# Row maximum over 64 MB: four blocks with pitches of their own, and some rows by TensorE and GpSimd

## The chip, the cores and the metric

The kernel runs on one core of a Trainium2 chip. The metric is the device time of one execution in microseconds; the comparison is by medians of several executions.

## The reference

The input is `x`, float32, 32 x 512 x 1024, drawn from a normal distribution. The output is the maximum over the last axis:

```python
def reference(x):
    return np.max(x, axis=-1).astype(np.float32)      # (32, 512)
```

Flattened, these are 16,384 rows of 1,024 numbers, 4 KB each: 67.11 MB are read, 65 KB are written, and each number is looked at once.

## The kernel before

The 16,384 rows are dealt out to the 128 partitions so that each partition has 128 rows which lie together in memory (`xr`). Neighbouring partitions are therefore 128 x 4 KB = 512 KB apart in HBM. This distance is called the pitch here.

The loop over `ROWS` (27 entries, 10 and 13 rows at first, single rows at last) does three things for each entry `g`. It takes `g` places in `ring`, a tile of 46 rows per partition, and goes back to place 0 when they don't fit. It issues one load of `g` rows for all partitions from the queue of SyncE (SP), line 47. It issues one `reduce_max` on VectorE (DVE), line 48, which writes `g` columns of `res`. A load waits on SP until the instructions that read its places before have finished; a reduce waits for its load. SP and DVE each work in the order of the program, so nothing overtakes anything on either queue.

The last row is loaded and reduced in two halves (lines 58 and 59), which are joined by one small instruction (line 60). The results leave by two stores from the queue of ScalarE (ACT): the first 112 columns at line 53 as soon as they are there, the last 16 at line 64. TensorE (PE) has nothing to do, and GpSimd (POOL) only sets four constants at the start.

Of the kernel before, what the change touches and what calls it, by code (L numbers as in the profile page):

```python
# [1 line left out]

# [4 lines left out]


F32 = mybir.dt.float32


ROWS = [10, 13, 12, 10, 9, 8, 7, 7, 6, 5, 5, 4, 4, 3, 3, 3, 3, 2, 2, 2, 2, 2, 1, 1, 1, 1, 1]
RING = 46


@with_exitstack
def kernel(
    ctx: ExitStack,
    tc: tile.TileContext,
    x: bass.AP,  # L20
    out: bass.AP,
):
    nc = tc.nc
    P = 128
    X = mybir.AxisListType.X

    xf = x.flatten_outer_dims()
    N, D = xf.shape
    H = D // 2
    I = N // P  # L30

    xr = xf.rearrange("(p i) d -> p i d", p=P)
    of = out.flatten_outer_dims()
    out_r = bass.AP(tensor=of.tensor, offset=of.offset, ap=[[I, P], [1, I]])

    once = ctx.enter_context(tc.tile_pool(name="once", bufs=1))
    ring = once.tile([P, RING, D], F32)
    res = once.tile([P, I], F32)
    part = once.tile([P, 2], F32)

    b = at = 0
    stored = 0
    for g in ROWS:
        if at + g > RING:
            at = 0
        xc = ring[:, at:at + g, :]
        nc.sync.dma_start(out=xc, in_=xr[:, b:b + g, :])
        nc.vector.reduce_max(out=res[:, b:b + g], in_=xc, axis=X)  # L48
        at += g
        b += g  # L50
        if not stored and b >= I - 16:
            stored = b
            nc.scalar.dma_start(out=out_r[:, :b], in_=res[:, :b])

    assert b == I - 1 and at + 1 <= RING
    for h in range(2):
        xh = ring[:, at, h * H:(h + 1) * H]
        nc.sync.dma_start(out=xh, in_=xr[:, b, h * H:(h + 1) * H])
        nc.vector.reduce_max(out=part[:, h:h + 1], in_=xh, axis=X)  # L59
    nc.vector.tensor_tensor(  # L60
        out=res[:, b:b + 1], in0=part[:, 0:1], in1=part[:, 1:2],
        op=mybir.AluOpType.max,
    )
    nc.scalar.dma_start(out=out_r[:, stored:], in_=res[:, stored:])


# [1 line left out]
_INS = ['x']  # L68
_OUTS = [((32, 512), 'float32')]


# [23 lines left out]
```

## Time and profile before

| what | value |
|---|---|
| median of 8 executions | 166.87 us (166.26 to 167.31) |
| the profiled execution, its own time | 167.04 us |
| its span | 165.3 us |
| DVE busy | 139.4 us, 84% of the span, 30 instructions |
| bytes read | 67.11 MB, a mean of 406 GB/s over the span |

The span is what the profile covers; the own time has 1.74 us more, which lie around it. A busy share is an average over the whole span, so it doesn't tell which resource sets the pace of a stage. That is read from the waits and from the chain that ended last.

### The profile page before, as it was taken

What the parts mean: (1) busy time and instruction counts of PE and PEld (TensorE: products, weight loads), DVE (VectorE), ACT (ScalarE), POOL (GpSimd) and SP (SyncE); (2) the same over time, 40 slices, a digit from 0 to 9 for tenths busy, and PEclk for the clock granted to TensorE, in tenths of its full rate; (3) what the DMA queues carried; (4) which work ended last, traced back from release to release, by engine and by line L of the source; (5) the groups of instructions that cost most, each with busy time, mean ns of one, the idle gap of its engine ahead of it and who ended that gap; (6) DMA issues with size and microseconds to landing.
All of it is one profiled execution on the core that took longest, in us unless ns stands there. A gap on an engine that the chain in (4) does not pass through costs nothing.

```text
span 165.3 us, 118 instructions
## 1 busy us (share of the span) xinstructions
DVE 139.4 (84%) x30; POOL 0.2 (0%) x4
## 2 busy tenths in 40 slices
DVE  0001994399989999899999989999999999999994
POOL 0000000000000000000000000000000000000000
DMA  5999999989999999999999999999999999999970
GB/s 198 436 476 391 464 438 451 445 381 428 442 436 406 460 357 419 413 420 439 430 437 423 429 432 425 436 426 419 436 420 422 422 425 421 418 422 419 408 280 2
DMA packets 4464, 67.18 MB, mean 406 GB/s; under 512 B 752, under 2 KB 752, under 8 KB 1648
## 3 DMA queue, kind: packets, MB, share of 16 engines
q1 hardware_dynamic: 4176, 67.11, 95.6%
q10 hardware_dynamic: 288, 0.07, 0.2%
HBM read 67.11 MB, written 0.07 MB: 406 GB/s over the span
## 4 chain that ended last, share of the span: by engine, by line
DMA 70%; DVE 28%; issue 0%
DMA ring<-in_x_dram 70%; DVE res L48 27%; DVE part L59 1%; DVE res L60 0%
## 5 line engine op out<-in xcount | busy, mean ns | idle before, releaser
L48 DVE TENSOR_REDUCE res<-ring 128x2 f32<-128x2048 f32 (+11 forms) x27 | 138.1, 5165 | 23.5 <-DMA ring<-in_x_dram 23.3
L59 DVE TENSOR_REDUCE part<-ring 128x1 f32<-128x512 f32 x2 | 1.3, 675 | 0.0
L60 DVE TENSOR_TENSOR res<-part 128x1 f32<-128x1 f32 x1 | 0.2, 158 | 0.0
L79 POOL MEMSET const-uint8-127<- 128x1 uint8 x1 | 0.1, 103 | 0.0
L79 POOL MEMSET const-bfloat16-1.0<- 128x1 bf16 x1 | 0.1, 102 | 0.0
L79 POOL MEMSET const-float32-0.0<- 128x1 f32 x1 | 0.1, 99 | 0.2 <-issue 0.2
L79 POOL MEMSET const-float32-1.0<- 128x1 f32 x1 | 0.1, 99 | 0.0
## 6 DMA issues: line engine op xcount, KB each, us to landing
ring<-in_x_dram SPq DMA_DIRECT2D x2, 5120.0 KB, 35.5
ring<-in_x_dram SPq DMA_DIRECT2D x2, 3584.0 KB, 33.6
ring<-in_x_dram SPq DMA_DIRECT2D x1, 6656.0 KB, 30.3
ring<-in_x_dram SPq DMA_DIRECT2D x1, 6144.0 KB, 44.4
ring<-in_x_dram SPq DMA_DIRECT2D x4, 1536.0 KB, 38.9
ring<-in_x_dram SPq DMA_DIRECT2D x2, 2560.0 KB, 38.4
ring<-in_x_dram SPq DMA_DIRECT2D x5, 1024.0 KB, 22.2
ring<-in_x_dram SPq DMA_DIRECT2D x1, 4608.0 KB, 43.7
```

The costliest lines, as they stand in the source:

```text
L48: nc.vector.reduce_max(out=res[:, b:b + g], in_=xc, axis=X)
L59: nc.vector.reduce_max(out=part[:, h:h + 1], in_=xh, axis=X)
L60: nc.vector.tensor_tensor(out=res[:, b:b + 1], in0=part[:, 0:1], in1=part[:, 1:2], op=mybir.AluOpType.max,)
L79: nc = _bacc.Bacc("TRN2", target_bir_lowering=False, num_devices=1)
```

## The change

**Blocks.** The rows are cut into four blocks, by the code of 42, 36, 34 and 16 rows per partition (the short description names 42, 35, 34 and 17). Within a block each partition again has rows that lie together, so the pitch is 168, 144, 136 and 64 KB. Each block has a store of its own, from the ACT queue. The ring has 42 places in place of 46. The 25 loads are those in `BLOCKS`; the last row isn't halved any more.

**The other way.** Each entry `(n, m)` of `BLOCKS` is one load of `n` rows, of which the last `m` don't go to the large `reduce_max`. There are 14 such rows of 128: six loads of the first blocks carry 2, 2, 2, 2, 2 and 1 of them, three more carry 1 each. Such a row takes this way, in `by_gpsimd`:

```python
for c in range(C):                                  # C = 8
    nc.tensor.transpose(out=ps[:, c*P:(c+1)*P],
        in_=rows[:, k, c*P:(c+1)*P], identity=ident)          # L63, PE
nc.scalar.copy(out=sb, in_=ps)                                # L69, ACT
nc.gpsimd.partition_all_reduce(top, sb, P, bass_isa.ReduceOp.max)   # L71, POOL
...
nc.tensor.transpose(out=back[:, k, c:c + 1],                  # L76, PE, 8 of them
    in_=top[0:1, c*P:(c+1)*P], identity=ident[0:1, 0:1])
...
nc.vector.reduce_max(out=cols, in_=back, axis=X)              # L83, DVE
```

Eight 128 x 128 blocks are turned, so that the numbers of one row lie across the partitions; ACT takes them from PSUM to SBUF; POOL takes the maximum over the partitions; eight small transposes bring the result back to one number per partition and block, and a small `reduce_max`, called the merge from here on, takes the maximum of the eight. There are three `ps` buffers, and two each of `sb`, `top` and `back`.

The diff, cut to its core:

```diff
-ROWS = [10, 13, 12, 10, 9, 8, 7, 7, 6, 5, 5, 4, 4, 3, 3, 3, 3, 2, 2, 2, 2, 2, 1, 1, 1, 1, 1]
-RING = 46
+BLOCKS = [
+    [(14, 2), (14, 2), (14, 2)],
+    [(14, 2), (13, 2), (9, 1)],
+    [(7, 1), (8, 1), (6, 1), (5, 0), (3, 0), (3, 0), (2, 0)],
+    [(2, 0), (2, 0), (2, 0), (2, 0), (1, 0), (1, 0), (1, 0), (1, 0), (1, 0), (1, 0), (1, 0), (1, 0)],
+]
+RING = 42
...
+    at = first = 0
+    for loads in BLOCKS:
+        S = sum(n for n, m in loads)
+        xb = xf[first * P:(first + S) * P, :].rearrange("(p i) d -> p i d", p=P)
+        b = 0
+        for n, m in loads:
+            if at + n > RING:
+                at = 0
+            xc = ring[:, at:at + n, :]
+            nc.sync.dma_start(out=xc, in_=xb[:, b:b + n, :])
+            cols = res[:, first + b:first + b + n]
+            if m:
+                merge = by_gpsimd(xc[:, n - m:, :], cols[:, n - m:], m)
+            else:
+                run(backs)
+            nc.vector.reduce_max(out=cols[:, :n - m], in_=xc[:, :n - m, :], axis=X)
+            run(late)
+            if m:
+                late.append(merge)
...
+        late.append(store)
+        first += S
+    run(late)
```

The program is written with the merges and the small transposes put off by one load and one row. The instructions of the built kernel stand in another order, since its scheduler sorts them. On DVE and PE the built kernel has, for the first two loads (the others likewise):

```
DVE  L104 reduce of load 0, 12 rows    (waits for load 0)
     L83  merge of load 0              (waits for PE)
     L104 reduce of load 1, 12 rows    (waits for load 1)
     L83  merge of load 1              (waits for PE)
PE   L63  16 transposes of load 0      (waits for load 0)
     L76  8 + 8 small transposes of load 0   (each 8 wait for POOL)
     L63  16 transposes of load 1      (waits for load 1)
     L76  8 + 8 small transposes of load 1   (each 8 wait for POOL)
```

After the ninth merge DVE has 16 reduces of loads without a row for POOL: 5, 3, 3, five times 2, and eight times 1 row.

More of the change, by code (lines that the diff above doesn't have):

```diff
@@ L6 @@
 from concourse._compat import with_exitstack
+from concourse import bass_isa
+from concourse.masks import make_identity
 F32 = mybir.dt.float32
-ROWS = [10, 13, 12, 10, 9, 8, 7, 7, 6, 5, 5, 4, 4, 3, 3, 3, 3, 2, 2, 2, 2, 2, 1, 1, 1, 1, 1]
-RING = 46
+BLOCKS = [
[5 more added lines that the diff above has]
+RING = 42
 @with_exitstack
@@ L28 @@
     N, D = xf.shape
-    H = D // 2
+    C = D // P
     I = N // P
-    xr = xf.rearrange("(p i) d -> p i d", p=P)
     of = out.flatten_outer_dims()
-    out_r = bass.AP(tensor=of.tensor, offset=of.offset, ap=[[I, P], [1, I]])
     once = ctx.enter_context(tc.tile_pool(name="once", bufs=1))
+    turn = ctx.enter_context(tc.tile_pool(name="turn", bufs=2))
+    allr = ctx.enter_context(tc.tile_pool(name="allr", bufs=2))
+    psum = ctx.enter_context(tc.tile_pool(name="psum", bufs=3, space=bass.MemoryType.PSUM))
@@ L37 @@
+    psmall = ctx.enter_context(tc.tile_pool(name="psmall", bufs=2, space=bass.MemoryType.PSUM))
     ring = once.tile([P, RING, D], F32)
     res = once.tile([P, I], F32)
[L39 to L64, printed above, removed]
+    ident = once.tile([P, P], F32)
+    make_identity(nc, ident)
@@ new lines, with by_gpsimd, turn_back @@
+    backs = []
+    late = []
+    def by_gpsimd(rows, cols, m):
+        back = psmall.tile([P, m, C], F32)
+        for k in range(m):
+            ps = psum.tile([P, D], F32)
+            for c in range(C):
+                nc.tensor.transpose(
+                    out=ps[:, c * P:(c + 1) * P],
+                    in_=rows[:, k, c * P:(c + 1) * P],
+                    identity=ident,
+                )
+            sb = turn.tile([P, D], F32)
+            nc.scalar.copy(out=sb, in_=ps)
+            top = allr.tile([P, D], F32)
+            nc.gpsimd.partition_all_reduce(top, sb, P, bass_isa.ReduceOp.max)
+            run(backs)
+            def turn_back(top=top, k=k):
+                for c in range(C):
+                    nc.tensor.transpose(
+                        out=back[:, k, c:c + 1],
+                        in_=top[0:1, c * P:(c + 1) * P],
+                        identity=ident[0:1, 0:1],
+                    )
+            backs.append(turn_back)
+        return lambda: nc.vector.reduce_max(out=cols, in_=back, axis=X)
@@ new lines, in run, with store @@
+    def run(calls):
+        while calls:
+            calls.pop(0)()
+    at = first = 0
[12 more added lines that the diff above has]
+            else:
+                run(backs)
+            nc.vector.reduce_max(out=cols[:, :n - m], in_=xc[:, :n - m, :], axis=X)
+            run(late)
+            if m:
+                late.append(merge)
+            at += n
+            b += n
+        def store(first=first, S=S):
+            dst = bass.AP(tensor=of.tensor, offset=of.offset + first * P, ap=[[S, P], [1, S]])
+            nc.scalar.dma_start(out=dst, in_=res[:, first:first + S])
+        late.append(store)
+        first += S
@@ L68 @@
+    run(late)
+    assert first == I
 _INS = ['x']
```

## The prediction

> **What bounds the kernel now.** I read the page's first two parts and then the time by stages: is anything saturated, and where?
>
> ```profile
> span 165.3 us, 118 instructions
> ...
> DVE 139.4 (84%) x30; POOL 0.2 (0%) x4
> ...
> GB/s 198 436 476 391 464 438 451 445 381 428 442 436 406 460 357 419 413 420 439 430 437 423 429 432 425 436 426 419 436 420 422 422 425 421 418 422 419 408 280 2
> ```
>
> ```profile
> 8.00:20.00 12.00, 4.23 (x1) 0.00 (x0) 1.00 1.00 431
> 20.00:40.00 20.00, 15.08 (x2) 0.00 (x0) 1.00 1.01 437
> ...
> 60.00:80.00 20.00, 19.38 (x2) 0.00 (x0) 1.00 0.97 411
> ...
> 140.00:150.00 10.00, 9.67 (x5) 0.00 (x0) 1.00 1.01 421
> ```
>
> In the second view the last two columns are the DMA engines' busy share and GB/s. From 4 us to 159 us the share is 0.97 or more: the loads set the pace. DVE is nearly as full in the second half (19.4 us of 20). The chain that ended last says the same: loads, then in the last 9 us DVE with no wait.
>
> ```profile
> 133.72 19.91 DMA ring<-in_x_dram
> ...
> 153.65 7.92 DVE res L48 x6
> 161.57 1.20 DVE part L59 x2
> ...
> 162.79 0.16 DVE res L60
> ```
>
> Two series of numbers come from here. First, when rows land. The timeline has the second reduce starting at 31.5 us (23 rows landed) and the third at 46.05 us (35 rows), both right after a wait for a load:
>
> ```profile
> 31.51 14.02 DVE L48 TENSOR_REDUCE res<-ring 128x13 f32<-128x13312 f32 x1 [4.92 <-DMA ring<-in_x_dram]
> 46.05 23.68 DVE L48 TENSOR_REDUCE res<-ring 128x12 f32<-128x12288 f32 x2 [0.52 <-DMA ring<-in_x_dram]
> 97.06 43.72 DVE L48 TENSOR_REDUCE res<-ring 128x7 f32<-128x7168 f32 x9 [0.81 <-DMA ring<-in_x_dram]
> ```
>
> (46.05 - 31.51) / 12 = 1.21 us per row; 97.06 us is 76 rows, 1.24 from there. I use **landing of n rows = 3.6 + 1.22 n us** (23 rows: 31.7). Second, what a reduce costs, from the groups kept apart by shape (busy, mean ns):
>
> ```profile
> L48 DVE TENSOR_REDUCE res<-ring 128x7 f32<-128x7168 f32 x2 | 15.2, 7616 | 0.8 <-DMA ring<-in_x_dram 0.8
> ...
> L48 DVE TENSOR_REDUCE res<-ring 128x3 f32<-128x3072 f32 x4 | 13.3, 3348 | 0.5 <-DMA ring<-in_x_dram 0.3
> L48 DVE TENSOR_REDUCE res<-ring 128x12 f32<-128x12288 f32 x1 | 13.0, 12954 | 0.5 <-DMA ring<-in_x_dram 0.5
> L48 DVE TENSOR_REDUCE res<-ring 128x2 f32<-128x2048 f32 x5 | 11.2, 2280 | 0.3 <-DMA ring<-in_x_dram 0.3
> L48 DVE TENSOR_REDUCE res<-ring 128x5 f32<-128x5120 f32 x2 | 11.0, 5480 | 0.0
> ...
> L48 DVE TENSOR_REDUCE res<-ring 128x1 f32<-128x1024 f32 x5 | 5.7, 1209 | 0.0
> ```
>
> So a row costs DVE 1.08 us in a large reduce and 1.21 us alone, against 1.22 us to load it.
>
> **What the Trainium skill says.** (1) "DMA: Bandwidth & Descriptors", Latency and other measured facts: copies between HBM tensors ran at 207 GB/s per direction with a 512 KiB pitch, at 214 with a padded one. The same page (Where 436 GB/s comes from) puts a core's ceiling at 435 GB/s. The trace doesn't show the loss: 431 and 437 GB/s at a pitch of 512 KB from 8 to 40 us; it falls to 411-430 later, where loads are smaller and one stage waits for the ring. (2) "GPSIMD Engine Reference", 3.2: a partition-axis reduce of 128 x 2048 took 247.7 us; 3.1: a loop of many operations runs at about 3 per cycle, a tight one at 1.8 cycles per element. No run here shows either. (3) "SBUF — State Buffer" says that on trn2 `tensor_reduce` never contends with GpSimd for the shared port, so I charge DVE nothing for POOL's work; the trace before can't show it.
>
> **The change, part by part.**
>
> *Blocks and pitch.* At the ceiling of 435 GB/s the 67.11 MB take 154.3 us, at the mean of 8 to 159 us (about 425) 157.9 us. A gain of 0 to 3.6 us on the loads, hence on each landing at most 2%. It counts only where DVE waits for loads at the end. I take 0. Two more stores: 0.4 us of ACT's queue each, beside other work. The last store has 16 columns as before, and the time from DVE's end to the span's end stays 165.3 - 162.95 = 2.35 us.
>
> *Work taken from DVE.* 14 rows at 1.08 = 15.1 us, less nine merges of about 0.2 us (line 60, the nearest small row, is 0.16), less what single rows cost more. DVE has about 127 us of work in place of 139.4. Off the path while loads set the pace.
>
> *Work added.* For each row of the other way:
> - 8 transposes. The skill ("TensorE: Matmul & The Clock Gate", Part 4) has 275 to 390 ns for one; in a stream they may overlap, so 0.9 to 3.1 us a row. I take 2.0.
> - The copy: "ScalarE: Activation LUTs" (What ACT_TABLE_LOAD costs) gives 186 ns + 0.833 ns per element, 1.04 us. The table load comes before the first landing.
> - POOL, **the number that decides, T**. From below: 1024 elements at 1.8 cycles and 1.2 GHz, 1.5 us. From above: half of 247.7, 124 us. My estimate from the same page: 16 lanes to one needs four steps of a move and a maximum (8 operations), with read, write and the exchange between cores about 14 per element, 4.7 cycles at the full 3 per cycle. A real loop will need 6 to 9: 5.1 to 7.7 us. I take the middle and 0.1 for dispatch, **T = 6.5 us**. The first call may pay about 6 us more (2.1), but POOL is free from some 10 us on and its first input comes at 24 us.
> - 8 small transposes: 0.5 to 2.2 us, taken as 1.0.
>
> *The wait that is added.* In the built order the merge of a load stands on DVE **ahead of** the next load's reduce, and PE's small transposes stand ahead of the next load's transposes. So DVE can't start the next reduce until POOL is done with this load, and the next load's POOL work can't start earlier either: the rows go round one circle, PE, ACT, POOL, PE, DVE. Its length: 2.0 + 1.04 + 1.0 + 0.2 + 0.2 for hand-overs = 4.4 us (3 to 6), plus T per row (a second row's transposes and copy lie under the first's T). That is **17.4 us for two rows, 10.9 for one**. The reduce of 12 rows, 13.0 us, lies inside it. Against it stand the landings, 17.1 us for 14 rows, 15.9 for 13, and then 11.0, 8.5, 9.8, 7.3 for 9, 7, 8, 6. So the circle keeps up at first and then falls behind. Start of a load's work is the later of its landing and the merge before:
>
> 20.7 (load 0 landed); merges at 38.1, 55.5, 72.9, 90.3, 107.7 (two rows each), then 118.6, 129.5, 140.4, 151.3. The ninth's rows had landed at 3.6 + 99 x 1.22 = 124.4. DVE then has 29 rows left, all but a few long landed (the last at 159.8): 5.48 + 2 x 3.35 + 5 x 2.28 + 8 x 1.21 = 33.3 us. DVE ends at 184.6, the span at 187.0, own time + 1.74 = 188.7. The profiled execution before was 0.17 above the median: **188.5 us**.
>
> *The ring.* SP now waits for PE as well as DVE. Tightest is the load of 8 rows, which needs the reduce of load 4 (90.3 + 11.9 = 102.2), while loads already issued last until 2 + 85 x 1.22 = 105.7. For a longer T the loads stall, but what is late next is DVE's queue anyway, so this costs nothing further.
>
> **Rivals.** *POOL is quick* (T up to 2 us). Then circles fit inside the reduces, and DVE sets the end from the landing of 93 rows (117.1): 7.6 + 5.5 + 0.4 + 33.3 = 163.9, time 167.8; with landings at 435 GB/s (1.205 us a row) 166.4, or less if small loads gain too. This ends at no change or slightly faster. For it: the page's 1.8 cycles for the simplest body. Against it: a maximum across lanes isn't that. It decides below about 2 us; at 3.4 us the last circles already are 7.8 long and the time is 170. *POOL is slow:* T = 9 gives circles of 22.4 and 13.4, 20.7 + 112 + 53.6 + 33.3 + 3.9 = 223.5; at the partition-axis price, 124 us, 14 rows give 1.8 ms. *The pitch does nothing:* likely, given 437 GB/s before, and it changes no sum above since DVE is late.
>
> **How the numbers follow.** The circle with T of 5 to 8: 0.87; POOL quick or nearly so: 0.07; POOL slow: 0.06. Ends: T = 5 gives 177 (the circle keeps up until load 4), T = 7.7 gives 205; the 4.4 us, nine times, may be 1.5 off either way, 13 us. Not all errors fall together: 174 to 207. By 0.3%, about what a measurement here can tell: faster 0.04, same 0.03, slower 0.93.
>
> **What would show it.** POOL at about 14 x 6.5 us busy; DVE idle before L83, released by PE, and that by POOL; DVE's last 33 us without waits; loads done well before the end. It's wrong if DVE's idle time before L83 is small, or if its last reduces wait for loads.

## The result, and the profile after

The changed kernel is slower, by far less than forecast: **168.63 us** (median of 11) against 166.55 us (median of 32 runs of the kernel before, the earlier eight among them); ratio 1.0124, 95% interval 1.0106 to 1.0142. In a later comparison on one chip it was 168.49 against 165.86 us, 1.016 (1.0146 to 1.0174). The two intervals don't overlap: the changed kernel took the same time in both, the kernel before 0.7 us more in the first, and why is open. The experiments are read against the later one. They ran on four chips, each beside the kernel before, whose median was 165.82 to 165.96 us there.

The first two parts of the page of the changed kernel (digits are busy tenths in 40 slices of 4.2 us):

```profile
span 167.0 us, 634 instructions
...
PE 40.1 (24%) x224; PEld 35.6 (21%) x224; DVE 124.5 (75%) x34; ACT 15.5 (9%) x15; POOL 45.8 (27%) x20
...
DVE  0000099919992899279938999996899599999994
...
POOL 0000019301930094009500944343073400000000
DMA  6999999999999999999999999999999999999900
```

DVE has 15 us less to do than before (124.5 against 139.4), and the loads are done one slice earlier. Still the span is 1.7 us longer. The DVE row says why it can be: the holes (1, 2, 3) lie in the first 21 slices, and from the 33rd on there are none.

The costliest groups (count | busy us, mean ns of one | idle before, releaser):

```profile
L104 DVE TENSOR_REDUCE res<-ring 128x1 f32<-128x1024 f32 (+8 forms) x25 | 124.0, 5009 | 38.3 <-DMA ring<-in_x_dram 38.3
L71 POOL PARTITION_ALL_REDUCE top<-sb x14 | 45.1, 3254 | 74.7 <-ACT sb L69 74.7
...
L69 ACT COPY sb<-ps 128x1024 f32<-128x1024 f32 x14 | 14.2, 1012 | 111.9 <-PE ps L63 111.9
...
L83 DVE TENSOR_REDUCE res<-back 128x2 f32<-128x16 f32 (+1 forms) x9 | 1.5, 163 | 1.8 <-PE back L76 1.8
```

The all-reduce took **3.22 us** (median; the mean is 3.25), where I had reckoned with 6.5. And the merges, which were to hold DVE up for tens of microseconds, held it up for 1.8 us, once. The timeline of DVE (start, us, instruction, idle before) and the chain that ended last show where:

```profile
115.43 0.16 DVE L83 TENSOR_REDUCE res<-back 128x1 f32<-128x8 f32 x1
117.57 7.62 DVE L104 TENSOR_REDUCE res<-ring 128x7 f32<-128x7168 f32 x1 [1.99 <-DMA ring<-in_x_dram]
125.15 0.17 DVE L83 TENSOR_REDUCE res<-back 128x1 f32<-128x8 f32 x1
125.23 5.47 DVE L104 TENSOR_REDUCE res<-ring 128x5 f32<-128x5120 f32 x1
132.53 0.17 DVE L83 TENSOR_REDUCE res<-back 128x1 f32<-128x8 f32 x1 [1.83 <-PE back L76]
132.62 31.97 DVE L104 TENSOR_REDUCE res<-ring 128x5 f32<-128x5120 f32 x16
```

```profile
100.37 17.18 DMA ring<-in_x_dram
...
117.68 1.96 PE ps L63 x8
...
119.72 1.02 ACT sb L69
120.74 0.08 issue
120.82 3.22 POOL top L71
...
128.16 3.28 POOLq L144
...
131.48 1.03 PE back L76 x8
132.51 0.02 issue
132.53 0.17 DVE res L83
132.70 28.51 DVE res L104 x13
```

The chain of the kernel before ran in loads until 153.65 us and then in DVE for 9.3 us. Now it leaves the loads at 117.55 us, goes twice round the circle (PE, ACT, POOL, PE, DVE), with the row of the load of 8 and then with that of the load of 6, and stays on DVE for the last 32 us. (The view follows the second turn only through POOL, as "issue" and "POOLq".) The turns join on PE:

```profile
124.10 1.01 PE L76 MATMUL back<-ident,top 1*128 1x1 f32 x8 [4.47 <-POOL top L71]
125.04 1.97 PE L63 MATMUL ps<-ident,ring 128*128 128x128 f32 x8
```

The load of 6 lands at about the same moment (in e9_finer_load below DVE waits for it until 124.50 us), so what counts is one turn of 7.5 us after that landing. The loads have nothing to say behind it any more: their last bytes came at about 159 us, DVE ended at 164.6.

### The profile page after: what moved, and what is told of

Read it like the earlier page. It is cut to its first block, busy times and chain, and to the rows that moved or that the text cites. A ratio compares the mean times of both kernels' runs of the same rounds, so it can differ in the third digit from the quotient of the medians.

```text
span 167.0 us, 634 instructions
## 1 busy us (share of the span) xinstructions
PE 40.1 (24%) x224; PEld 35.6 (21%) x224; DVE 124.5 (75%) x34; ACT 15.5 (9%) x15; POOL 45.8 (27%) x20
## 4 chain that ended last, share of the span: by engine, by line
DMA 55%; DVE 33%; issue 3%; POOLq 2%; POOL 2%; PE 2%; DVEq 1%; ACT 1%; SPq 0%; ACTq 0%
DMA ring<-in_x_dram 55%; DVE res L104 33%; POOLq L144 2%; POOL top L71 2%; PE ps L63 1%; DVEq L144 1%; PE back L76 1%; ACT sb L69 1%; SPq L98 0%; DVE res L83 0%; ACTq L69 0%
## 5 line engine op out<-in xcount | busy, mean ns | idle before, releaser
L104 DVE TENSOR_REDUCE res<-ring 128x1 f32<-128x1024 f32 (+8 forms) x25 | 124.0, 5009 | 38.3 <-DMA ring<-in_x_dram 38.3
L71 POOL PARTITION_ALL_REDUCE top<-sb x14 | 45.1, 3254 | 74.7 <-ACT sb L69 74.7
L63 PE MATMUL ps<-ident,ring 128*128 128x128 f32 x112 | 26.1, 424 | 49.6 <-DMA ring<-in_x_dram 49.6
L63 PEld LDWEIGHTS ps<-ident,ring 128*128 128x128 f32 x112 | 22.7, 226 | 50.0 <-issue 43.8
L69 ACT COPY sb<-ps 128x1024 f32<-128x1024 f32 x14 | 14.2, 1012 | 111.9 <-PE ps L63 111.9
L76 PE MATMUL back<-ident,top 1*128 1x1 f32 x112 | 14.1, 243 | 42.7 <-POOL top L71 42.7
L76 PEld LDWEIGHTS back<-ident,top 1*128 1x128 f32 x112 | 13.0, 214 | 46.8 <-POOL top L71 46.8
L83 DVE TENSOR_REDUCE res<-back 128x2 f32<-128x16 f32 (+1 forms) x9 | 1.5, 163 | 1.8 <-PE back L76 1.8
```

What stands on the lines that cost most here:

```text
L63: nc.tensor.transpose(out=ps[:, c * P:(c + 1) * P], in_=rows[:, k, c * P:(c + 1) * P], identity=ident,)
L69: nc.scalar.copy(out=sb, in_=ps)
L71: nc.gpsimd.partition_all_reduce(top, sb, P, bass_isa.ReduceOp.max)
L76: nc.tensor.transpose(out=back[:, k, c:c + 1], in_=top[0:1, c * P:(c + 1) * P], identity=ident[0:1, 0:1],)
L83: return lambda: nc.vector.reduce_max(out=cols, in_=back, axis=X)
L104: nc.vector.reduce_max(out=cols[:, :n - m], in_=xc[:, :n - m, :], axis=X)
```

## The experiments

Theory A after the result: the circle is as foreseen but quick; what sets the end is DVE's own work behind the last thing it waits for. Rival: the other way costs the time itself, merge after merge.

**One part alone: the pitch.** The kernel before with blocks of 45, 37, 30 and 16 rows and a store each; everything else as before.

```diff
-        nc.sync.dma_start(out=xc, in_=xr[:, b:b + g, :])
+        nc.sync.dma_start(out=xc, in_=rows(b, g))
...
+        xb = xf[f * P:(f + S) * P, :].rearrange("(p i) d -> p i d", p=P)
+        return xb[:, b - f:b - f + g, :]
```

> The kernel before with four blocks of 45, 37, 30 and 16 rows per partition (pitches of 180, 148, 120 and 64 KB) and a store for each; loads, ring and reduces as before, all on VectorE. Theory A (the pitch lets the loads run a little faster, but VectorE has only about 1.5 us of waits left from 97 us to its end, so it takes over as the bound): 165.2 us against 166.5, the last bytes about 1.3 us earlier, VectorE with next to no waits after 97 us. Rival (the pitch does nothing, what ended the loads earlier in the changed kernel was their size): 166.5 us.

Measured: 165.27 against 165.86 us, ratio 0.9964 (0.9952 to 0.9976). The gain is there, half of what was expected, and this is the one kernel here that is faster than both. The waits of DVE after 90 us fell to 0.9 us. Its chain has the same shape as before, 1.7 us earlier in this one execution (the profile of the kernel before is from the first comparison, where that kernel was 0.7 us slower):

```profile
132.12 19.83 DMA ring<-in_x_dram
151.95 0.02 issue
151.97 7.92 DVE res L60 x6
159.89 1.20 DVE part L70 x2
...
161.11 0.16 DVE res L71
```

**The other way alone:** the changed kernel at a pitch of 512 KB.

```diff
-        xb = xf[first * P:(first + S) * P, :].rearrange("(p i) d -> p i d", p=P)
+        xb = xr[:, first:first + S, :]
```

> The changed kernel with the rows dealt out at a pitch of 512 KB throughout (same loads, same rows to TensorE and GpSimd, four stores). Theory A (VectorE's tail starts when the load that completes 93 rows lands, and the pitch moves that landing by about 1 us): 169.6 us. Rival (pitch does nothing): 168.6 us, as the changed kernel.

Measured: 169.12 us, ratio 1.0191 (1.0178 to 1.0204); the changed kernel beside the same before median had 168.49. So the pitch is worth 0.6 us here too. The rate at which the first loads stream doesn't show it. Loads 0 and 1 of this kernel and of the changed kernel run again:

```profile
21.97 12.95 DVE L105 TENSOR_REDUCE res<-ring 128x12 f32<-128x12288 f32 x1 [21.97 <-DMA ring<-in_x_dram]
...
38.90 12.95 DVE L105 TENSOR_REDUCE res<-ring 128x12 f32<-128x12288 f32 x1 [3.89 <-DMA ring<-in_x_dram]
```

```profile
21.19 12.95 DVE L104 TENSOR_REDUCE res<-ring 128x12 f32<-128x12288 f32 x1 [21.19 <-DMA ring<-in_x_dram]
...
38.12 12.95 DVE L104 TENSOR_REDUCE res<-ring 128x12 f32<-128x12288 f32 x1 [3.90 <-DMA ring<-in_x_dram]
```

Both have 16.93 us from one landing to the next, whatever the pitch. In this pair the difference is in the first landing (0.78 us) and for the most part stays (0.66 us at the last merge). In the pair of e1_pitch_alone and the kernel before, 0.4 us lie in the first landing and more comes later. But these are single executions, and at the changed kernel's pitch the first landing itself lay between 20.81 us (e6_all_reduce_twice) and 22.13 (e4_last_four_only). So where the 0.6 us arise is open.

**No row the other way,** same loads: every `m` in `BLOCKS` set to 0.

> The changed kernel with no row sent to TensorE and GpSimd: VectorE reduces all 128 rows of the same 25 loads. Theory A (the end is VectorE's work after the load of 13 rows; only rows taken from it there count): 88.4 + 14.0 + 9.75 + 7.6 + 8.7 + 6.5 + 32.0 = 166.9 in place of 164.6, so 170.9 us. Rival (the other way itself costs the time, through its waits): faster than 168.6, near 166.5.

Measured: 169.33 us, ratio 1.0208 (1.0194 to 1.0221). Slower than the changed kernel, so the rival falls: the way doesn't cost more than it brings. It came out 1.6 us below the sum, and the trace shows why: its load of 13 rows landed at 87.05 us, where the sum had 88.4 (the changed kernel's). Of these 1.4 us, 0.6 lie in the first landing: kernels without GpSimd's work start sooner, see below. The rest came later.

Beside e1_pitch_alone, measured on the same chip, this run says more. In both DVE does all rows, without the all-reduce, at nearly the same pitches; what differs is the list of loads, with the ring of 42 places and the last row in one piece. Yet this one takes **4.06 us more** (169.33 against 165.27), which is more than the changed kernel loses in all. Its DVE starts later and never waits after 87 us:

```profile
20.43 15.09 DVE L104 TENSOR_REDUCE res<-ring 128x14 f32<-128x14336 f32 x1 [20.43 <-DMA ring<-in_x_dram]
...
87.05 78.16 DVE L104 TENSOR_REDUCE res<-ring 128x13 f32<-128x13312 f32 x21 [0.71 <-DMA ring<-in_x_dram]
```

In all DVE waits 26.7 us for loads, in e1_pitch_alone 21.6, and the 5.1 us between them lie in the first wait: 20.43 us for 14 rows, 15.35 for 10. That points to the larger first load; no run changes it alone.

**Ten of the fourteen rows back to DVE.**

```diff
-    [(14, 2), (14, 2), (14, 2)],
-    [(14, 2), (13, 2), (9, 1)],
+    [(14, 0), (14, 0), (14, 0)],
+    [(14, 0), (13, 0), (9, 1)],
```

> The changed kernel with only the last four of the 14 rows sent to TensorE and GpSimd (those of the loads of 9, 7, 8 and 6 rows); the first ten go back to VectorE, 2 in each of the first five loads. Theory A (VectorE idles 3.5 to 3.9 us before each of these loads' successors, more than the 2.2 us that two rows cost, so ten of the fourteen rows buy nothing): 168.6 us, within 0.3 of the changed kernel. Rival (all relief of VectorE counts): later by up to 10 x 1.08 = 10.8 us, 179 us.

Measured: 168.38 us, ratio 1.0152 (1.0129 to 1.0175), with the changed kernel's 168.49 within the uncertainty. **Ten rows, 10.8 us of DVE's work, buy nothing,** to within about 0.4 us. They are taken from DVE where it has waits for loads to spare, and the last wait of DVE is for the same merge (132.81 us here, 132.53 there).

**The merges behind.** DVE's instructions are held in the written order.

```diff
-            nc.vector.reduce_max(out=cols[:, :n - m], in_=xc[:, :n - m, :], axis=X)
+            pin(nc.vector.reduce_max(out=cols[:, :n - m], in_=xc[:, :n - m, :], axis=X))
...
-        return lambda: nc.vector.reduce_max(out=cols, in_=back, axis=X)
+        return lambda: pin(nc.vector.reduce_max(out=cols, in_=back, axis=X))
```

> The changed kernel with VectorE's instructions held in the written order, so that each merge stands behind the next load's reduce. Theory A (POOL's circle costs VectorE only the one wait of 1.83 us before the last merge; the rest of the loss is VectorE's own work after the last large load): 1.8 us less than the changed kernel, ratio to before 1.001. Rival (the loss is the circle, merge after merge): well below the kernel before, 0.99 or less.

The changed kernel was run beside it:

> The changed kernel as it is, on the chip of this group, so that the others can be read against it: ratio to the kernel before 1.012 as in the first comparison, by every theory.

It had 168.49 us, ratio 1.016. With the merges behind: 167.07 us, ratio 1.0075 (1.0061 to 1.0089), 1.42 us less, where 1.8 were expected. The wait for POOL is gone, and a short wait for a load has taken a little of its place:

```profile
130.10 0.15 DVE L84 TENSOR_REDUCE res<-back 128x1 f32<-128x8 f32 x1
130.55 5.49 DVE L105 TENSOR_REDUCE res<-ring 128x5 f32<-128x5120 f32 x1 [0.29 <-DMA ring<-in_x_dram]
```

**POOL made twice as slow:** each all-reduce is issued twice. This is the prediction's own case, a row at 6.45 us.

```diff
             nc.gpsimd.partition_all_reduce(top, sb, P, bass_isa.ReduceOp.max)
+            nc.gpsimd.partition_all_reduce(top, sb, P, bass_isa.ReduceOp.max)
```

> The changed kernel with each partition_all_reduce done twice, the second time over the same input into the same tile, so that a row costs POOL 6.45 us in place of 3.22. Theory A (the circle is right, only T was wrong): two rows 4.35 + 4 x 3.22 = 17.2 us, one row 10.8; merges at 38.3, 55.5, 72.7, 90.0, 107.2, 118.0, 128.8, 139.6, 150.4, then 32.0 of VectorE and 4.1 around: 186.5 us. Rival (POOL runs beside the rest and is hidden): 168.6 us, or about 172 if only the last wait grows.

Measured: **186.6 us**, ratio 1.1251 (1.1235 to 1.1266). Who waited for whom in this kernel (us in total, times, longest):

```profile
DVE res L84 <- PE back L77: 36.4, 9, 5.3
...
DVE res L105 <- DMA ring<-in_x_dram: 20.8, 1, 20.8
```

All nine merges wait now, and no reduce after the first waits for a load. The circle is real; it needs a slower POOL to fall behind.

**Fewer rows, later:** the loads and pitches of e1_pitch_alone, one row each out of the loads of 7, 6, 5, 5, 4 and 4 rows.

```diff
+AWAY = (7, 8, 9, 10, 11, 12)
...
+        m = 1 if j in AWAY else 0
+        if m:
+            merge = away(xc[:, g - 1, :], res[:, b + g - 1:b + g])
```

> The kernel with the pitches of e1_pitch_alone, its loads and its halved last row; six single rows go to TensorE and GpSimd, out of the loads of 7, 6, 5, 5, 4 and 4 rows in the middle, and each merge stands behind the next load's reduce; ring of 45 places. Theory A (VectorE was the bound at the end with 9.3 us of work without a wait; six rows are 6.5 us of relief where it has no other slack, and the last landing takes over): 164.5 us, ratio 0.991 (e1_pitch_alone had 0.9964). Rival (the end is the loads' already, or POOL's work slows the loads): 165.3 us or more, no faster than e1_pitch_alone.

Measured: 172.82 us, ratio 1.0415 (1.0401 to 1.043): a miss by 8 us. The order built for PE put each row's small transposes ahead of the next row's large ones. The chain of this kernel, one turn:

```profile
118.63 1.92 PE ps L70 x8
...
120.63 1.02 ACT sb L72
...
121.73 3.23 POOL top L74
...
125.01 1.01 PE back L77 x8
126.01 1.92 PE ps L70 x8
```

One turn takes 7.4 us (118.63 to 126.01), the loads landed some 5 us apart. With PE's order changed (the small transposes of a row, and with them its merge, behind the large ones of the next):

```diff
-            nc.tensor.transpose(out=ps[:, c * P:(c + 1) * P], in_=row[:, c * P:(c + 1) * P], identity=ident)
+            pin(nc.tensor.transpose(out=ps[:, c * P:(c + 1) * P], in_=row[:, c * P:(c + 1) * P], identity=ident))
...
+        turn_back()
```

> The kernel e7_fewer_later with TensorE's instructions held in an order in which the small transposes of a row stand behind the large ones of the next. Theory A (e7 lost its time because six rows, 5 us apart, went round a circle of 7.4 us, since each row's large transposes stood behind the small ones of the row before; with the order changed that is gone, but six rows of relief before 150 us buy nothing, as VectorE waits for the load that lands at 152 us all the same): ratio 0.9964, as e1_pitch_alone, where e7 had 1.0415. Rival (the relief counts): 0.99. Second rival (something else in e7 cost the time): above 1.02.

Measured: 166.4 us, ratio 1.0033 (1.0021 to 1.0046). So the order on PE had cost 6.4 us. What stays is 1.1 us above e1_pitch_alone, though DVE has six rows less.

**One row, where it should count:** only the last load of two rows gives one away. The edit is against e7_fewer_later; the ring has its 46 places again, and the merge stands after the last whole row.

```diff
-AWAY = (7, 8, 9, 10, 11, 12)
+AWAY = (21,)
```

> The kernel e1_pitch_alone with a single row to TensorE and GpSimd, out of the last load of two rows, which lands at about 152 us; its merge stands before the two half rows. Theory A (VectorE last waits for that load and then works 9.3 us without a wait, so that only relief after it counts; the row's way of 7.5 us fits into it): 0.9 us less than e1_pitch_alone, ratio to before 0.991. Rival (the last landing sets the end, or the way is longer than the stretch): 0.9964 as e1_pitch_alone, or a little more.

Measured: 166.23 us, ratio 1.0025 (1.0014 to 1.0037), also about 1 us above e1_pitch_alone: a miss, for two reasons. The first is that the row's relief brought hardly anything. From the landing of that load to DVE's end it is 9.08 us in place of 9.30, because with one row less DVE catches up with the loads and then waits a little for the single rows behind: its six reduces start 1.28 us apart, in e1_pitch_alone the single rows 1.12. The chain now runs in the loads until 159.09 us:

```profile
152.72 7.62 DVE L90 TENSOR_REDUCE res<-ring 128x1 f32<-128x1024 f32 x6 [0.20 <-DMA ring<-in_x_dram]
```

```profile
150.23 8.86 DMA ring<-in_x_dram
...
159.12 1.22 DVE res L90
```

So the rival of this run, that the last landing sets the end, is right here. The second reason is that its loads landed later from the first on (15.77 us in place of 15.35 for 10 rows; the load it gives a row from at 152.72 in place of 151.97), long before a row is sent away at 152 us. That points to what every kernel with GpSimd's work does at the start.

**Only the set-up:** e1_pitch_alone with the identity and one all-reduce of it, read by nobody.

```diff
+    make_identity(nc, ident)
+    nc.gpsimd.partition_all_reduce(top, ident, P, bass_isa.ReduceOp.max)
```

> The kernel e1_pitch_alone with only GpSimd's set-up added: the identity and one partition_all_reduce of it, whose result nobody reads; no row is sent away. Theory A (starting the way delays the first loads by 0.4 to 1 us, and that delay stays to the end): ratio to before 1.001, 0.8 us over e1_pitch_alone, first 10 rows landed at about 15.8 us in place of 15.35. Rival (the delay comes from the rows sent away, or from nothing but chance): 0.9964, as e1_pitch_alone.

Measured: 166.48 us, ratio 1.0029 (1.0014 to 1.0044), 0.65% above e1_pitch_alone, **about 1.1 us**. The two ran on different chips, each beside the kernel before; e8_one_row_last and e10_six_in_order, on a third, lie 0.6% and 0.7% above e1_pitch_alone. Ten rows landed at 16.10 us in place of 15.35 (first line: e1_pitch_alone, second: this kernel), and the load that DVE waits for last at 153.11 in place of 151.97:

```profile
15.35 10.82 DVE L60 TENSOR_REDUCE res<-ring 128x10 f32<-128x10240 f32 x1 [15.35 <-DMA ring<-in_x_dram]
```

```profile
16.10 10.82 DVE L67 TENSOR_REDUCE res<-ring 128x10 f32<-128x10240 f32 x1 [16.10 <-DMA ring<-in_x_dram]
```

POOL itself stands still for 10.85 us before the identity can be finished:

```profile
0.72 0.20 POOL masks.py:197 MEMSET ident<- 128x128 f32 x1 [0.29 <-POOLq L97]
11.78 0.28 POOL masks.py:199 TENSOR_SCALAR_AFFINE_SELECT ident<-ident 128x128 f32<-128x128 f32 x1 [10.85 <-issue]
22.17 0.72 POOL L59 PARTITION_ALL_REDUCE top<-ident  x1 [10.11 <-issue]
```

The kernel without a row for POOL, e3_blocks_no_way, made the same identity at 1.00 us. So POOL's standstill belongs to the all-reduce, not to the identity. The loads fit that: the first load of 14 rows landed at 20.43 us in e3_blocks_no_way and at 20.81 or later in each of the seven kernels here that have the same first load and pitch and the all-reduce. Why loads issued by SP are delayed the profile doesn't show.

**A finer load, then a finer tail,** both on e5_merges_behind: `(8, 1)` becomes `(4, 0), (4, 1)`; then also

```diff
-... (6, 1), (5, 0), (3, 0), (3, 0), (2, 0)],
+... (6, 1), (3, 0), (3, 0), (3, 0), (2, 0), (2, 0)],
```

> The kernel e5_merges_behind with the load of 8 rows in the third block cut into two of 4 (the row to GpSimd from the second). Theory A (VectorE idles about 2 us for that load, and everything behind it is VectorE's own work without a wait): 2 us less than e5_merges_behind, 165.0 us, ratio 0.995, about that of e1_pitch_alone. Rival (the loads, or something at the end, sets the time): no change, 1.0075.

> The kernel e9_finer_load with the four loads after the 99th row, of 5, 3, 3 and 2 rows, cut into 3, 3, 3, 2 and 2. Theory B (the end is the landing of the last load that VectorE waits for and its own work from there; e9 only moved a 2.3 us wait from the load of 8 rows to the load of 5 rows that lands at 130.6, and with a load of 3 there VectorE starts 2.3 us earlier and stays ahead): 1.7 us less than e9_finer_load, 165.3 us, ratio 0.997. Rival (something common to these kernels sets the end): 1.0076, as e9_finer_load.

Measured: the first 167.06 us, ratio 1.0076 (1.0064 to 1.0089), no change: a miss. DVE's wait of 2.0 us for the load of 8 is gone, but DVE now waits for the two loads behind it, 1.8 us (until 124.50) for that of 6 rows and 0.55 for the next of 5, until the same moment as before. The chain says so too:

```profile
100.69 29.89 DMA ring<-in_x_dram
130.58 0.02 issue
130.60 5.49 DVE res L105
```

The second 166.39 us, ratio 1.0029 (1.0018 to 1.0039): 0.8 us less by the ratios, half of what was expected, as the load of 6 rows before it now holds DVE until 124.39 us.

All of these can be read in one way: **DVE's end is the last thing that it waits for, plus its work from there.** That holds of any engine by the meaning of the words, so it proves nothing; what it gives is the place to look, and a change moves that place. Before: 153.65 + 9.3 = 162.95 us. e1_pitch_alone: 151.97 + 9.3. e5_merges_behind: 130.55 + 32.05 = 162.60. e13_finer_tail: 124.39 + 37.57 = 161.96. The changed kernel has the wait for a merge as its last, 132.53 + 32.06 = 164.59. In e8_one_row_last the relief itself moved the last wait to the single row that came at 159.1 us.

## Why the prediction was wrong

**The step that failed is the one marked as deciding, T,** POOL's time for a row: 6.5 us taken, 3.22 measured. With it fell what the forecast rested on, a circle that falls behind load after load. The prediction's own sign of being wrong came, DVE's idle time before L83 being small: 1.8 us, once. With the slow POOL of e6_all_reduce_twice the circle did what the prediction says, so the wait was rightly seen and its size wrong.

The forecast was a slower kernel because of the circle. It is slower, but mostly because of something else, the list of loads; that the direction came out right is to that extent luck. Two of the signs that were to show the circle, DVE's last stretch without waits and loads done before the end, came too, but in e3_blocks_no_way, which has no circle, DVE is without waits from 87 us on. The change in steps:

| step | us | difference |
|---|---|---|
| the kernel before | 165.86 | |
| pitch (e1_pitch_alone) | 165.27 | -0.59 |
| list of loads, ring of 42, whole last row (e3_blocks_no_way) | 169.33 | +4.06 |
| 14 rows by the other way (the changed kernel) | 168.49 | -0.84 |

The last step is on another chip than the first three, with the same median of the kernel before. In it the other way as a whole gains. Two costs are inside it: the merges' place in DVE's order, 1.42 us (the changed kernel over e5_merges_behind), and the set-up, some 1.1 us if it costs here what it cost in e11_setup_only. The prediction had the new loads in its sum, through the landings and DVE's last 29 rows, but not as a cost of their own.

- *T.* I had counted 14 operations per element, 4.7 cycles at the best, from the rate that the Trainium skill gives ("GPSIMD Engine Reference", 3.1). 3.22 us for 1,024 elements are 3.8 cycles at the 1.2 GHz that I had used: below what I took for the floor. The two bounds, 1.5 and 124 us, held it; the estimate within them was worth nothing, and the range should have reached down towards the value at which no wait is left.
- *The circle around T.* Forecast 4.4 us. Measured on the last row of the changed kernel: from 125.04 to 132.51 us, 7.47 us, less 3.22 is 4.25. Its parts: large transposes 1.94 (taken as 2.0), copy 1.01 (1.04), small transposes 1.01 (1.0), merge 0.17 (0.2). With 3.22 for T my formula gives the last five merges at 99.9, 108.8, 116.4, 124.9, 132.5; the trace has 100.22, 108.90, 115.43, 125.15, 132.53. (The third is earlier because PE is free for the next row before DVE has done the merge, which the formula doesn't allow.) The whole sum then gives about 169.7 us, for 168.6 measured. That 2.0 was so near for the large transposes is in part luck: the skill's price ("TensorE: Matmul & The Clock Gate", Part 4) is for bf16, and 2.0 was picked within 0.9 to 3.1. With T doubled on the chip the time was 186.6 us, where I had 188.5 for T = 6.5.
- *Landings.* 20.7, 37.8 and 117.1 us forecast, 21.05, 37.98 and 117.57 measured.
- *DVE's last 29 rows.* 33.3 us forecast, 32.06 measured: I added durations, and consecutive reduces overlap by some 0.08 us.
- *The cover.* The rival "POOL is quick" had the right picture: with circles inside the reduces DVE's own work sets the end, and at a T of 3.4 us only the last circles are longer, with a time of 170. But the case "quick or nearly so" had a chance of 0.07, and the range began at 174.
- *Pitch.* Taken as 0 of 0 to 3.6 us; 0.6 us measured, in e1_pitch_alone and again between e2_way_alone and the changed kernel. That it changes no sum "since DVE is late" was thus not right: in that pair of executions the last merge came at 132.75 and 132.09 us. The loss that the skill has for copies between HBM tensors ("DMA: Bandwidth & Descriptors", Latency and other measured facts) doesn't appear in the rate of the first loads: 16.93 us per 14 rows at either pitch.
- *Set-up.* I had costed POOL's start at nothing, since POOL is idle then. For POOL that was right, though the start was longer than the some 6 us that I had from the skill ("GPSIMD Engine Reference", 2.1): 10.41 us of standstill in the changed kernel, in e11_setup_only 10.85 and another 10.11 before the first all-reduce. But the loads paid too: 1.1 us in e11_setup_only, which nothing covers.
- *No contention.* The reduce of 12 rows took 12.953 us beside POOL's work and 12.954 in the kernel before, as the skill says ("SBUF — State Buffer", Who interferes with whom).

## What to carry to other kernels

Relief of an engine counts only behind the last thing it waits for: find that moment in the chain, and price a move by what it takes away after it; ten of fourteen moved rows were worth nothing here. It counts, too, only until the next thing that the engine will wait for: one row taken where nothing waited brought 0.2 us of its 1.1. When a change has several parts, run the plain ones alone: here a new list of loads, which looked like a side matter, cost 4.06 us and hid that the rest gained. And when one unknown price decides, take the range from the point at which it stops mattering to its bound, not from the middle of an estimate.

## What the runs showed that I had not expected

- `partition_all_reduce` on 128 x 1024 float32 takes 3.22 us, on 128 x 128 0.72 us.
- In kernels that use it POOL stands still for 10 to 11 us near the start, and the first load of another queue landed 0.4 us or more later than in the one kernel with the same loads and pitch and no all-reduce (single executions).
- Eight transposes of 128 x 128 float32 took 1.96 us with a recorded TensorE clock of 1.00 (the changed kernel) and of 0.50 (the same kernel run again): the recorded clock made no difference to them.
